# The gate's modulation summed on VectorE alone, with the low parts of the weights on GpSimd, in the last two stages

## The chip, the cores and the metric

The kernel runs on one core of a Trainium2 chip. The metric is the device time of one execution in microseconds (us); lower is better. Before the change three runs gave a median of 1195.83 us (1193.9 to 1196.08).

## What is computed

One step of a diffusion backbone over 384 tokens of width 2048 (256 of a sample, 128 of a prompt): an adaLN modulation, one wide projection, a state-space branch and an attention branch, and a gated way back. The last part of it is what the change is about:

```
mod = silu(cond) @ w_ada + b_ada             # cond: 2 vectors; w_ada: 2048 x 6144
shift, scale, gate = split(mod, 3)           # gate: the last 2048 columns of w_ada
...
p_s = ys @ w_ssm_out
p_a = (attn * silu(z_a)) @ w_att_out         # the stage `pa`
merged = sigmoid(g_s) * p_s + sigmoid(g_a) * p_a
return x + gate * (merged @ w_o)             # the stage `wo`
```

All of it is in float32.

## The kernel before

**Products in three parts.** TensorE multiplies float32 by splitting each operand into a high part (rounded to the engine's fast float32 form, `F32R`) and a low part (the rest), and adds three products: high x high, high x low, low x high. The high and low parts of the activations are made once (`hh`, `hl`). Those of the weights are made as they stream in, by `Stream.prep` (L59 to L72): ScalarE copies a piece of 128x512 into `hi` (L70), and VectorE or GpSimd subtracts it from the raw piece to give `lo` (L71), GpSimd where the flag `low_on_pool` is set. The flag is set in the first stage and cleared after it (L895, L949).

**Stages.** After the first stage the work is a list of `blocks`, of which the last are `ps` (8 blocks), `pa` (8) and `wo` (4). A block is made of units of weights (one DMA of 512 KB each, four raw buffers), a unit of two halves; one half is called a step here. A `pa` step is 12 matmuls on 128x384 in `mode_b` (L192 to L194), first the six for one PSUM bank, then the six for the other; a `wo` step is 9 matmuls on 128x512 in `mode_a` (L203 to L205), three for each of three banks. A `pa` block has 4 steps, a `wo` block 16, so the gate's step counter `t` runs from 0 to 31 in `pa` and from 32 to 95 in `wo`. The pool `psm` of the products has three banks, `psb` for everything else five. The weights are prepared two steps ahead (`st.upto`, L1445), into four buffers of `hi` and four of `lo`.

**What VectorE evicts.** At the end of a `pa` block (`evac`) VectorE twice computes `tgl = (tgl + 1) * PSUM` and adds it to `ms`, the merged activations; later `split` makes `hh` and `hl` of `ms`. At the end of a `wo` block it multiplies three banks by the gate `gt` into `yt` and adds the input `xt`.

**The gate before.** `gate_step(t)` (L1348) is called once a step in these stages. The first 1024 columns of the gate are summed on TensorE: eight groups of four float32 matmuls with the two conditioning vectors (`ct`, 32 columns wide) as the stationary operand, each of the four in another 32 rows of one bank (L1379); `gate_rows` then adds the bias (`bg`), splits the result and spreads it over the 128 partitions with matmuls by `sel` (L1399). The other 1024 columns are summed on VectorE: for each of 16 blocks of 128 rows of `w_ada` and each of the two vectors one `scalar_tensor_tensor` on 128x512, `acs = gw * ct + acs` (L1365, recorded as L155, the line of the helper); `gate_sums` splits `acs` and spreads and sums it over the partitions with matmuls by a matrix of ones (L1416). The table `GATE` gives the step of each of these 32 blocks, from 26 to 84.

**Order.** Each engine runs its instructions in the order in which the program is written; loads are issued from SyncE's queue, also in order. Generators in `Background` (merging, gate sums) advance by one `yield` a step. The helpers `tt`, `ts` and `stt` (L146 to L155) record VectorE's instructions under their own lines.

Of the kernel before, what the change touches and what calls it, by code (L numbers as in the profile page):

```python
# [6 lines left out]
F32 = mybir.dt.float32  # L7
F32R = mybir.dt.float32r
I32 = mybir.dt.int32
AF = mybir.ActivationFunctionType  # L10
OP = mybir.AluOpType
AX = mybir.AxisListType
# [3 lines left out]
D = 2048  # L16
# [10 lines left out]
def f(ap):  # L27
    return ap.bitcast(F32)


def dram(ap, off, dims):
    return bass.AP(tensor=ap.tensor, offset=ap.offset + off, ap=[list(d) for d in dims])
# [94 lines left out]
def hybrid(ctx, tc, a):  # L127
    nc = tc.nc
    V, S, PE, GP, SP = nc.vector, nc.scalar, nc.tensor, nc.gpsimd, nc.sync
# [13 lines left out]
    def bank():  # L143
        return psb.tile([128, 512], F32, name="bk")

    def tt(o, x, y, op, eng=V):  # L146
        return eng.tensor_tensor(o, x, y, op=op)  # L147

    def ts(o, x, s1, op0, s2=None, op1=None, eng=V):
        if op1 is None:  # L150
            return eng.tensor_scalar(o, x, s1, None, op0=op0)
        return eng.tensor_scalar(o, x, s1, s2, op0=op0, op1=op1)  # L152

    def stt(o, x, s, y, op0, op1):
        return V.scalar_tensor_tensor(o, x, s, y, op0=op0, op1=op1)  # L155
# [740 lines left out]
    i = 0  # L896
# [333 lines left out]
    def enter(kind):  # L1230
        nonlocal kvt
        if kind == "v":
            bg.finish(g_zs)
            zsx.close()
            v = vx.enter_context(pool("vp"))
            M["v"] = [v.tile([128, 1024], F32, name=f"v{r}") for r in range(4)]
            SP.dma_start(M["v"][3], dram(a["cache_v"], 0, [[1024, 128], [1, 1024]]))
        elif kind == "ga":
            pre = prex.enter_context(pool("pre"))
            for k, dims in (("B", [2, 32, 16]), ("C", [4, 2, 2, 64]), ("U", [16, 96]), ("D", [16, 16])):  # L1240
                prefetched[k] = pre.tile([128] + dims, F32, name="pre" + k)
            g_pre.append(bg.add(ssm_read(1, prefetched), True))
        elif kind == "k":
            bg.finish([g_ssm])
            sspx.close()
            prex.close()
            msp = ent(pool("msp", "right"))
            M["ms"] = [msp.tile([128, TOK], F32, name=f"ms{k}") for k in range(16)]
            ts(qwc, qwc, 0.125, OP.mult)
            kv = kvx.enter_context(pool("kv", "right"))  # L1250
            M["kS"] = [kv.tile([128, 384], F32, name=f"kS{j}") for j in range(8)]
            M["kP"] = [kv.tile([128, 128], F32, name=f"kP{j}") for j in range(8)]
            M["qT"] = [kv.tile([128, 384], F32, name=f"qT{j}") for j in range(8)]
            at = atx.enter_context(pool("at", "right"))
            kvt = kvtx.enter_context(pool("kvt", bufs=2))
            g_qk.append(bg.add(context_keys()))
            M["att"] = bg.add(attention(at, M["kS"], M["kP"], M["qT"], M["v"], M["qT"],
                                      M["vd"], M["aT"]))
        elif kind == "act":
            M["zs"], M["ys"] = {}, {}  # L1260
            M["ysg"] = bg.add(split_ys(), True)
        elif kind == "glu":
            bg.finish([M["ysg"]])
            for k in range(2):
                load_glu(k)
        elif kind == "ps":
            bg.finish(g_qk)
            kvtx.close()
            g_za.append(bg.add(gate_att(), True))
        elif kind == "pa":  # L1270
            bg.finish([M["att"]] + g_za)
            atx.close()
            kvx.close()
            vx.close()
            M["gp"] = gp = gx.enter_context(pool("gp", "right"))
            M["gt"] = gp.tile([128, 2, D], F32, name="gt")

            pick = gp.tile([128, 2], F32, name="pick")
            V.tensor_reduce(pick, ident.rearrange("p (g x) -> p x g", x=32)[:, 0:2], axis=AX.X, op=OP.add)
            M["sel"] = gp.tile([128, 3, 128], F32R, name="sel")  # L1280
            V.tensor_copy(M["sel"][:, 0:2], pick.unsqueeze(2).to_broadcast([128, 2, 128]))
            ts(M["sel"][:, 2], ident, 0.0, OP.mult, 1.0, OP.add)
            M["bg"] = gp.tile([128, D], F32, name="bg")
            GP.memset(M["bg"], 0.0)
            for n in range(2):
                SP.dma_start(M["bg"][0:2 - n, 1024 * n:1024 * n + 1024], dram(a["b_ada"], 4096 + 1024 * n, [[0, 2 - n], [1, 1024]]))
            M["tg"] = []
            for k in range(2):
                load_tg(k)
        elif kind == "wo":  # L1290
            g_mg.append(bg.add(merge(range(8, 16), 3), True))
# [55 lines left out]

    def gate_step(t):  # L1348

        for kt in range(32):
            if GATE[kt] - 6 == t and kt % 2 == 0:
                w = gaw[16 + kt // 2] = M["gp"].tile([128, 2, 512], F32, name="gw", bufs=5)
                n, k = divmod(kt, 16)
                SP.dma_start(w, dram(a["w_ada"], 128 * k * 6144 + 5120 + 512 * n, [[6144, 128], [128 * 6144, 2], [1, 512]]))
            if GATE[kt] == t:
                n, k = divmod(kt, 16)  # L1360
                if k == 0:
                    gaw["acc"] = M["gp"].tile([128, 2, 512], F32, name="acs", bufs=1)
                for m in range(2):
                    o = gaw["acc"][:, m]
                    stt(o, gaw[16 + kt // 2][:, kt % 2], ct[:, k, m:m + 1],  # L1365
                        o if k else M["bg"][:, 1024 + 512 * n:1536 + 512 * n], OP.mult, OP.add)
                if k == 15:
                    bg.add(gate_sums(2 + n, gaw["acc"]), True)
        if t % 2 == 0 and t < 32:
            w = gaw[t // 2] = M["gp"].tile([128, 2, 512], F32, name="gw", bufs=5)  # L1370
            n, u = divmod(t // 2, 8)
            SP.dma_start(w, dram(a["w_ada"], 256 * u * 6144 + 4096 + 512 * n, [[6144, 128], [128 * 6144, 2], [1, 512]]))
        quad, r = divmod(t - 8, 4)
        if r == 0 and 0 <= quad < 8:
            n, u = divmod(quad, 4)
            if u == 0:
                gaw["p"] = bank()
            for g in range(4):
                PE.matmul(gaw["p"][32 * g:32 * g + 32, :], ct[:, 4 * u + g, :], gaw[2 * quad + g // 2][:, g % 2],  # L1379
                          start=u == 0, stop=u == 3)  # L1380
            if u == 3:
                bg.add(gate_rows(n, gaw["p"]), True)

    def gate_rows(n, p):

        acc = M["gp"].tile([128, 512], F32, name="acc", bufs=1)
        h = M["gp"].tile([128, 512], F32R, name="gh", bufs=2)
        l = M["gp"].tile([128, 512], F32R, name="gl", bufs=2)
        yield -1
        tt(acc, p, M["bg"][:, 512 * n:512 * n + 512], OP.add)  # L1390
        yield -1
        S.activation(h, acc, AF.Copy)
        yield -1
        tt(l, acc, f(h), OP.subtract)
        for m in range(2):
            yield -1
            p = bank()
            for i, part in enumerate((h, l)):
                PE.matmul(p, M["sel"][:, m], part, start=i == 0, stop=i == 1)  # L1399
            yield -1  # L1400
            S.activation(M["gt"][:, m, 512 * n:512 * n + 512], p, AF.Copy)

    def gate_sums(n, acc):

        parts = []
        for m in range(2):
            parts.append([M["gp"].tile([128, 512], F32R, name=x, bufs=2) for x in ("gh", "gl")])
            S.activation(parts[m][0], acc[:, m], AF.Copy)
        yield -1
        for m in range(2):  # L1410
            tt(parts[m][1], acc[:, m], f(parts[m][0]), OP.subtract)
        for m in range(2):
            yield -1
            p = bank()
            for i, part in enumerate(parts[m]):
                PE.matmul(p, M["sel"][:, 2], part, start=i == 0, stop=i == 1)  # L1416
            yield -1
            S.activation(M["gt"][:, m, 512 * n:512 * n + 512], p, AF.Copy)

    gaw = {}  # L1420
    GATE = [26 + k * 60 // 32 for k in range(32)]
    BUD = {"gs": 2.05, "v": 2.1, "ga": 2.05, "za": 2.05}
    ACT = {"glu": act, "pa": act, "ps": act2, "wo": merged}
    entered, gt_ = set(), 0
    for kind, c0, nk, units in blocks:
        if kind not in entered:
            enter(kind)
            entered.add(kind)
# [58 lines left out]
```

## Time and profile before

| what | value |
|---|---|
| median of three runs | 1195.83 us |
| the profiled execution, its own time | 1188.56 us |
| its span, first to last instruction | 1186.8 us |
| mean granted clock of TensorE | 0.997 |
| TensorE (PE) busy | 1144.7 us, 96% |
| VectorE (DVE) busy | 834.2 us, 70% |
| ScalarE (ACT) busy | 519.6 us, 44% |
| GpSimd (POOL) busy | 176.3 us, 15% |

The profile is of one execution. Busy times are shares of the whole span and hide that stages have different limits. TensorE's matmuls are pipelined, so a matmul's own length (0.33 us on 128x384) is about twice the distance to the next one. PEld are TensorE's weight loads, which overlap its matmuls. In the rows, a line such as `acs<-gw,ct,acs` names the tile written and the tiles read. Tiles `m` and `bk` are in PSUM, all others here in SBUF.

### The profile page before, as it was taken

What the parts mean: (1) busy time and instruction counts of PE and PEld (TensorE: products, weight loads), DVE (VectorE), ACT (ScalarE), POOL (GpSimd) and SP (SyncE); (2) the same over time, 40 slices, a digit from 0 to 9 for tenths busy, and PEclk for the clock granted to TensorE, in tenths of its full rate; (3) what the DMA queues carried; (4) which work ended last, traced back from release to release, by engine and by line L of the source; (5) the groups of instructions that cost most, each with busy time, mean ns of one, the idle gap of its engine ahead of it and who ended that gap; (6) DMA issues with size and microseconds to landing.
All of it is one profiled execution on the core that took longest, in us unless ns stands there. A gap on an engine that the chain in (4) does not pass through costs nothing.

```text
span 1186.8 us, 19637 instructions
## 1 busy us (share of the span) xinstructions
PE 1144.7 (96%) x7215; PEld 1011.2 (85%) x7215; DVE 834.2 (70%) x1960; ACT 519.6 (44%) x978; POOL 176.3 (15%) x150
## 2 busy tenths in 40 slices
PE   4899999999999999999999999998999999999997
PEld 3699999998998888989999888876787998878886
DVE  4465555666899984789998533587788756687873
ACT  4343333354643356463335644556444433343332
POOL 2356555663100000000000001110100000000000
PEclk9999999999999999999999999999999999999999
DMA  9987777568456476427444264446553258886771
GB/s 307 323 267 230 253 250 248 156 170 228 156 125 188 134 150 154 129 83 175 148 155 142 72 200 138 116 132 221 161 163 124 93 167 266 273 293 218 222 231 66
DMA packets 216116, 217.37 MB, mean 183 GB/s; under 512 B 64618, under 2 KB 170690, under 8 KB 215637
## 3 DMA queue, kind: packets, MB, share of 16 engines
q1 hardware_dynamic: 213940, 212.73, 59.3%
q0 software_dynamic: 1184, 3.18, 0.8%
q8 instruction: 57, 0.93, 0.3%
q10 hardware_dynamic: 896, 0.21, 0.1%
q14 instruction: 39, 0.31, 0.1%
HBM read 197.90 MB, written 16.87 MB: 181 GB/s over the span
## 4 chain that ended last, share of the span: by engine, by line
PE 87%; DVE 5%; ACT 3%; DMA 2%; issue 2%; SPq 1%; POOL 0%; ACTq 0%; DVEq 0%; POOLq 0%
PE m L192 11%; PE m L194 11%; PE m L193 11%; PE m L203 9%; PE m L204 9%; PE m L205 9%; PE m L861 6%; PE m L862 5%; PE m L863 5%; PE bk L733 2%; PE bk L478 1%; PE bk L604 1%; PE bk L607 1%; PE bk L1032 1%; DMA raw<-in_w_in_dram 1%
## 5 line engine op out<-in xcount | busy, mean ns | idle before, releaser
L70 ACT ACTIVATE hi<-raw 128x512 fp32r<-128x512 f32 x464 | 287.4, 629 | 338.8 <-PE m L193 123.9
L71 DVE TENSOR_TENSOR lo<-raw,hi 128x512 fp32r<-128x512 f32 x368 | 250.2, 687 | 154.2 <-ACT hi L70 151.3
L192 PE MATMUL m<-hh,hi 128*128 128x384 f32 x832 | 285.3, 343 | 10.7 <-DVE ms L155 2.9
L194 PE MATMUL m<-hh,lo 128*128 128x384 f32 x832 | 278.9, 335 | 0.2
L193 PE MATMUL m<-hl,hi 128*128 128x384 f32 x832 | 278.4, 335 | 0.0
L203 PE MATMUL m<-hi,hh 128*128 128x512 f32 x480 | 189.9, 396 | 0.0
L205 PE MATMUL m<-hi,hl 128*128 128x512 f32 x480 | 187.3, 390 | 0.0
L204 PE MATMUL m<-lo,hh 128*128 128x512 f32 x480 | 187.1, 390 | 0.0
L192 PEld LDWEIGHTS m<-hh,hi 128*128 128x128 f32 x832 | 156.2, 188 | 22.7 <-ACT hi L70 5.4
L194 PEld LDWEIGHTS m<-hh,lo 128*128 128x128 f32 x832 | 156.2, 188 | 0.9 <-DVE lo L71 0.9
L193 PEld LDWEIGHTS m<-hl,hi 128*128 128x128 f32 x832 | 156.3, 188 | 0.1
L71 POOL TENSOR_TENSOR lo<-raw,hi 128x512 fp32r<-128x512 f32 x96 | 124.5, 1307 | 111.4 <-ACT hi L70 107.2
L861 PE MATMUL m<-hh,hi 128*128 128x384 f32 x384 | 132.8, 346 | 5.1 <-DVE ua L925 2.6
L863 PE MATMUL m<-hh,lo 128*128 128x384 f32 x384 | 129.3, 337 | 0.2 <-DVE lo L71 0.2
L862 PE MATMUL m<-hl,hi 128*128 128x384 f32 x384 | 129.2, 336 | 0.3 <-POOL hl L147 0.3
L203 PEld LDWEIGHTS m<-hi,hh 128*128 128x128 f32 x480 | 90.1, 188 | 21.5 <-ACT hi L70 1.4
L205 PEld LDWEIGHTS m<-hi,hl 128*128 128x128 f32 x480 | 90.1, 188 | 19.1
L204 PEld LDWEIGHTS m<-lo,hh 128*128 128x128 f32 x480 | 90.2, 188 | 18.1 <-DVE lo L71 0.3
L861 PEld LDWEIGHTS m<-hh,hi 128*128 128x128 f32 x384 | 72.5, 189 | 14.0 <-issue 5.7
L862 PEld LDWEIGHTS m<-hl,hi 128*128 128x128 f32 x384 | 72.6, 189 | 0.8 <-POOL hl L147 0.5
L863 PEld LDWEIGHTS m<-hh,lo 128*128 128x128 f32 x384 | 72.5, 189 | 0.4 <-DVE lo L71 0.4
L147 POOL TENSOR_TENSOR rm<-rn,mhalf 128x24 f32<-128x24 f32 x4 | 18.1, 4512 | 355.0 <-DVE rn L152 355.0
(270 smaller groups left out, 1274.0 us busy)
## 6 DMA issues: line engine op xcount, KB each, us to landing
raw<-in_w_in_dram SPq DMA_DIRECT2D x160, 512.0 KB, 3.9
wa<-in_w_ada_dram SPq DMA_DIRECT2D x32, 1024.0 KB, 7.7
gw<-in_w_ada_dram SPq DMA_DIRECT2D x32, 512.0 KB, 5.6
raw<-in_w_o_dram SPq DMA_DIRECT2D x32, 512.0 KB, 6.2
raw<-in_w_ssm_out_dram SPq DMA_DIRECT2D x16, 512.0 KB, 3.4
raw<-in_w_att_out_dram SPq DMA_DIRECT2D x16, 512.0 KB, 5.6
raw<-in_w_glu_dram SPq DMA_DIRECT2D x8, 512.0 KB, 4.5
tgs<-sg SPq DMA_DIRECT2D x16, 192.0 KB, 1.9
```

Of the source, the lines that this page charges most:

```text
L70: self.nc.scalar.activation(h, t, AF.Copy)
L71: (self.nc.gpsimd if self.low_on_pool else self.nc.vector).tensor_tensor(l, t, f(h), op=OP.subtract)
L192: PE.matmul(o, wh[:, kk, w], xh[q][:, j, :], start=first and hb == 0 and kk == 0, stop=False)
L193: PE.matmul(o, wh[:, kk, w], xl[q][:, j, :], start=False, stop=False)
L194: PE.matmul(o, wl[:, kk, w], xh[q][:, j, :], start=False, stop=last and hb == 1 and kk == 1)
L203: PE.matmul(ps[r], xh[q][:, j, tk], wh, start=first and hb == 0, stop=False)
L204: PE.matmul(ps[r], xh[q][:, j, tk], wl, start=False, stop=False)
L205: PE.matmul(ps[r], xl[q][:, j, tk], wh, start=False, stop=last and hb == 1)
L733: PE.matmul(pab[b][32 * (k % 4):32 * (k % 4) + 32, 0:128 * nk], ct[:, kt, :], wa[s, i][:, k, :], start=kt < 4, stop=kt >= 12)
L861: PE.matmul(o, wh[:, w], hh[q][:, j, :], start=kk == 0, stop=False)
L862: PE.matmul(o, wh[:, w], hl[q][:, j, :], start=False, stop=False)
L863: PE.matmul(o, wl[:, w], hh[q][:, j, :], start=False, stop=kk == nk - 1)
```

## The change

The whole gate, all 2048 columns, is now summed on VectorE: 64 blocks of rows and columns, two instructions each, spread by a new table `GATE` over steps 6 to 87. The products on TensorE, `gate_rows` and the two columns of `sel` that it used are gone; the matrix of ones is a tile of its own (`one`). The gate's loads, 32 of 512 KB as before, are all issued six steps ahead of the first use. The flag `low_on_pool` is set in `pa` and `wo`, so GpSimd makes the low parts there. The flag also stands in the budget that `bg.step` is given, which is 1 a step now and was 0.4.

```diff
-            M["sel"] = gp.tile([128, 3, 128], F32R, name="sel")
...
+            M["one"] = gp.tile([128, 128], F32R, name="one")
+            ts(M["one"], ident, 0.0, OP.mult, 1.0, OP.add)
             M["bg"] = gp.tile([128, D], F32, name="bg")
             GP.memset(M["bg"], 0.0)
...
+            SP.dma_start(M["bg"][0:1], dram(a["b_ada"], 4096, [[0, 1], [1, D]]))
...
     def gate_step(t):
-        for kt in range(32):
+        for kt in range(64):
+            n, k = divmod(kt, 16)
             if GATE[kt] - 6 == t and kt % 2 == 0:
...
             if GATE[kt] == t:
...
                 for m in range(2):
                     o = gaw["acc"][:, m]
-                    stt(o, gaw[16 + kt // 2][:, kt % 2], ct[:, k, m:m + 1],
-                        o if k else M["bg"][:, 1024 + 512 * n:1536 + 512 * n], OP.mult, OP.add)
+                    stt(o, gaw[kt // 2][:, kt % 2], ct[:, k, m:m + 1],
+                        o if k else M["bg"][:, 512 * n:512 * n + 512], OP.mult, OP.add)
                 if k == 15:
-                    bg.add(gate_sums(2 + n, gaw["acc"]), True)
-        if t % 2 == 0 and t < 32:
...
-            for g in range(4):
-                PE.matmul(gaw["p"][32 * g:32 * g + 32, :], ct[:, 4 * u + g, :], gaw[2 * quad + g // 2][:, g % 2],
-                          start=u == 0, stop=u == 3)
...
+                    bg.add(gate_sums(n, gaw["acc"]), True)
...
-                PE.matmul(p, M["sel"][:, 2], part, start=i == 0, stop=i == 1)
+                PE.matmul(p, M["one"], part, start=i == 0, stop=i == 1)
...
-    GATE = [26 + k * 60 // 32 for k in range(32)]
+    GATE = [6 + k * 80 // 64 + (k // 16) for k in range(64)]
...
     for kind, c0, nk, units in blocks:
+        st.low_on_pool = kind in ("pa", "wo")
```

The order of the instructions at three places follows. First VectorE in `pa`, between the evictions of the fourth block and the fifth, before:

```order
L147 TENSOR_TENSOR ms_7904<-ms_7904,tgl 128x384
L155 SCALAR_TENSOR_TENSOR tgl<-tgl,m 128x384
L147 TENSOR_TENSOR ms_7905<-ms_7905,tgl 128x384
L71 TENSOR_TENSOR lo<-raw,hi 128x512 x3
L155 SCALAR_TENSOR_TENSOR hl_105<-ms_7904,hh_101 128x384
L71 TENSOR_TENSOR lo<-raw,hi 128x512
L155 SCALAR_TENSOR_TENSOR hl_105<-ms_7905,hh_101 128x384
L155 SCALAR_TENSOR_TENSOR tgl<-tgl,m 128x384
```

and at the same place now:

```order
L147 TENSOR_TENSOR ms_7904<-ms_7904,tgl 128x384
L155 SCALAR_TENSOR_TENSOR tgl<-tgl,m 128x384
L147 TENSOR_TENSOR ms_7905<-ms_7905,tgl 128x384
L155 SCALAR_TENSOR_TENSOR acs<-gw,ct,acs 128x512 x6
L155 SCALAR_TENSOR_TENSOR hl_105<-ms_7904,hh_101 128x384
L155 SCALAR_TENSOR_TENSOR acs<-gw,ct,acs 128x512 x2
L155 SCALAR_TENSOR_TENSOR hl_105<-ms_7905,hh_101 128x384
L155 SCALAR_TENSOR_TENSOR tgl<-tgl,m 128x384
```

Four lows have gone from between the two evictions, and eight gate sums stand there. Second, VectorE in `wo`, from the eviction of its first block to that of its second, now:

```order
L147 TENSOR_TENSOR yt<-m,gt 128x512 x3
L147 TENSOR_TENSOR yt<-yt,xt 128x512 x3
L155 SCALAR_TENSOR_TENSOR acs<-gw,ct,bg 128x512 x2
L155 SCALAR_TENSOR_TENSOR acs<-gw,ct,acs 128x512 x24
L147 TENSOR_TENSOR yt<-m,gt 128x512 x3
```

Before, 16 lows stood among fewer gate sums there; now 26 gate sums stand between two evictions with nothing else. Third, the end of GpSimd's queue, as a piece of the difference (- before, + now):

```order
 L147 TENSOR_TENSOR rm<-rn,mhalf 128x24 x4
-L1284 MEMSET bg 128x2048
-L1483 UNCONDITIONAL_BRANCH
-L1483 ISA
+L1280 MEMSET bg 128x2048
+L71 TENSOR_TENSOR lo<-raw,hi 128x512 x94
```

GpSimd had nothing to do after the clearing of `bg`; it now makes 94 lows.

## Rows read from the trace of the kernel before

**Rows 1.** Busy in `pa`, `wo`: length; PE, PEld, DVE, ACT, POOL (count); granted clock; DMA

```profile
970.00:1044.00 74.00, 74.00 (x433) 67.29 (x433) 46.98 (x82) 25.76 (x46) 0.00 (x0) 1.00 0.81 262
1046.00:1179.00 133.00, 133.00 (x592) 108.26 (x592) 95.68 (x150) 44.51 (x73) 0.00 (x0) 1.00 0.63 207
```

**Rows 2.** VectorE groups from 964 us: line, instruction, count | busy, mean ns | idle, releaser

```profile
L71 DVE TENSOR_TENSOR lo<-raw,hi 128x512 fp32r<-128x512 f32 x96 | 64.7, 688 | 46.9 <-ACT hi L70 46.7
L155 DVE SCALAR_TENSOR_TENSOR acs<-gw,ct,acs 128x512 f32<-128x512 f32 x60 | 42.2, 745 | 0.0
L155 DVE SCALAR_TENSOR_TENSOR tgl<-tgl,m 128x384 f32<-128x384 f32 x16 | 8.8, 550 | 10.0 <-PE m L194 10.0
L147 DVE TENSOR_TENSOR yt<-m,gt 128x512 f32<-128x512 f32 x12 | 8.2, 692 | 8.2 <-PE m L205 8.2
```

**Rows 3.** TensorE in order of time, `pa`: start, length, instruction; eight matmul records of the gate

```profile
985.79 0.33 PE L192 MATMUL m<-hh,hi 128*128 128x384 f32 x1
...
987.35 0.33 PE L192 MATMUL m<-hh,hi 128*128 128x384 f32 x1
...
987.96 1.06 PE L1379 MATMUL bk<-gw,ct 128*32 128x512 f32 x8
...
990.65 0.33 PE L192 MATMUL m<-hh,hi 128*128 128x384 f32 x1
```

**Rows 4.** TensorE in order of time, `wo`

```profile
1051.40 0.39 PE L203 MATMUL m<-hi,hh 128*128 128x512 f32 x1
...
1053.44 0.39 PE L203 MATMUL m<-hi,hh 128*128 128x512 f32 x1
```

**Rows 5.** Groups of the spreading matmuls, from 964 us to the end

```profile
L1399 PE MATMUL bk<-gh,sel 128*128 128x512 f32 x4 | 1.7, 418 | 0.0
L1416 PE MATMUL bk<-gh,sel 128*128 128x512 f32 x4 | 1.6, 391 | 0.0
```

**Rows 6.** The page: loads of the gate weights, count, size, us to landing

```profile
gw<-in_w_ada_dram SPq DMA_DIRECT2D x32, 512.0 KB, 5.6
```

**Rows 7.** GpSimd, then VectorE, in order of time, first stage

```profile
266.02 1.30 POOL L71 TENSOR_TENSOR lo<-raw,hi 128x512 fp32r<-128x512 f32 x1 [1.37 <-ACT hi L70]
266.39 1.34 DVE L155 SCALAR_TENSOR_TENSOR zs<-sg,zs 128x384 f32<-128x384 f32 x1
```

**Rows 8.** GpSimd, then VectorE, in order of time, 210 to 218 us

```profile
214.27 1.62 POOL L71 TENSOR_TENSOR lo<-raw,hi 128x512 fp32r<-128x512 f32 x1
214.27 2.98 POOL L71 TENSOR_TENSOR lo<-raw,hi 128x512 fp32r<-128x512 f32 x2
213.40 1.32 DVE L147 TENSOR_TENSOR cm<-fw,pw 128x384 f32<-128x384 f32 x1
215.58 0.52 DVE L147 TENSOR_TENSOR fw<-fw,cm 128x192 f32<-128x192 f32 x1
```

**Rows 9.** VectorE, then GpSimd, in order of time, 61 to 64 us

```profile
61.88 2.06 DVE L147 TENSOR_TENSOR zs<-m,zs 128x384 f32<-128x384 f32 x4
61.93 1.29 POOL L71 TENSOR_TENSOR lo<-raw,hi 128x512 fp32r<-128x512 f32 x1 [3.71 <-ACT hi L70]
```

**Rows 10.** Pairs of VectorE instructions that follow each other, in order of time

```profile
978.75 1.28 DVE L71 TENSOR_TENSOR lo<-raw,hi 128x512 fp32r<-128x512 f32 x2
1060.28 1.41 DVE L155 SCALAR_TENSOR_TENSOR acs<-gw,ct,acs 128x512 f32<-128x512 f32 x2
```

**Rows 11.** VectorE, then TensorE, in order of time, 892 to 895 us

```profile
893.47 1.00 DVE L155 SCALAR_TENSOR_TENSOR ms<-ms,m 128x384 f32<-128x384 f32 x2
894.06 0.44 PE L192 MATMUL m<-hh,hi 128*128 128x384 f32 x1 [2.90 <-DVE ms L155]
```

**Rows 12.** A pause of TensorE, and its granted clock (PEclk) after it

```profile
32.37 0.69 PE L861 MATMUL m<-hh,hi 128*128 128x384 f32 x1 [2.63 <-DVE ua L925]
32.00:34.00 2.00, 1.64 (x5) 0.56 1.09 349
34.00:36.00 2.00, 2.00 (x22) 0.59 1.10 354
```

More of the change, by code (lines that the diff above doesn't have):

```diff
@@ L1276, in enter @@
             M["gt"] = gp.tile([128, 2, D], F32, name="gt")
-            pick = gp.tile([128, 2], F32, name="pick")
-            V.tensor_reduce(pick, ident.rearrange("p (g x) -> p x g", x=32)[:, 0:2], axis=AX.X, op=OP.add)
-            M["sel"] = gp.tile([128, 3, 128], F32R, name="sel")
-            V.tensor_copy(M["sel"][:, 0:2], pick.unsqueeze(2).to_broadcast([128, 2, 128]))
-            ts(M["sel"][:, 2], ident, 0.0, OP.mult, 1.0, OP.add)
+            M["one"] = gp.tile([128, 128], F32R, name="one")
+            ts(M["one"], ident, 0.0, OP.mult, 1.0, OP.add)
             M["bg"] = gp.tile([128, D], F32, name="bg")
             GP.memset(M["bg"], 0.0)
-            for n in range(2):
-                SP.dma_start(M["bg"][0:2 - n, 1024 * n:1024 * n + 1024], dram(a["b_ada"], 4096 + 1024 * n, [[0, 2 - n], [1, 1024]]))
+            SP.dma_start(M["bg"][0:1], dram(a["b_ada"], 4096, [[0, 1], [1, D]]))
             M["tg"] = []
@@ L1348, in gate_step @@
     def gate_step(t):
-        for kt in range(32):
+        for kt in range(64):
+            n, k = divmod(kt, 16)
             if GATE[kt] - 6 == t and kt % 2 == 0:
-                w = gaw[16 + kt // 2] = M["gp"].tile([128, 2, 512], F32, name="gw", bufs=5)
-                n, k = divmod(kt, 16)
-                SP.dma_start(w, dram(a["w_ada"], 128 * k * 6144 + 5120 + 512 * n, [[6144, 128], [128 * 6144, 2], [1, 512]]))
+                w = gaw[kt // 2] = M["gp"].tile([128, 2, 512], F32, name="gw", bufs=5)
+                SP.dma_start(w, dram(a["w_ada"], 128 * k * 6144 + 4096 + 512 * n, [[6144, 128], [128 * 6144, 2], [1, 512]]))
             if GATE[kt] == t:
-                n, k = divmod(kt, 16)
                 if k == 0:
@@ L1364, in gate_step @@
                     o = gaw["acc"][:, m]
-                    stt(o, gaw[16 + kt // 2][:, kt % 2], ct[:, k, m:m + 1],
-                        o if k else M["bg"][:, 1024 + 512 * n:1536 + 512 * n], OP.mult, OP.add)
+                    stt(o, gaw[kt // 2][:, kt % 2], ct[:, k, m:m + 1],
+                        o if k else M["bg"][:, 512 * n:512 * n + 512], OP.mult, OP.add)
                 if k == 15:
-                    bg.add(gate_sums(2 + n, gaw["acc"]), True)
-        if t % 2 == 0 and t < 32:
[L1370 to L1377, printed above, removed]
-            for g in range(4):
-                PE.matmul(gaw["p"][32 * g:32 * g + 32, :], ct[:, 4 * u + g, :], gaw[2 * quad + g // 2][:, g % 2],
-                          start=u == 0, stop=u == 3)
[L1381 to L1401, printed above, removed]
+                    bg.add(gate_sums(n, gaw["acc"]), True)
     def gate_sums(n, acc):
```

## The prediction

> **What bounds the kernel now.** Read the stages apart first. In `pa` and in `wo` TensorE is busy for the whole of both stretches, 74.00 of 74 us and 133.00 of 133 us, at a granted clock of 1.00 (the level of 2.4 GHz), while VectorE is busy for 46.98 and 95.68 us and GpSimd not at all [rows 1]. So in these two stages any time of TensorE that goes shortens the kernel, and work moved between VectorE and GpSimd is free only as long as neither makes TensorE wait. Then TensorE in order of time gives the lengths of a step (half a unit, twelve matmuls in `pa`, nine in `wo`). In `pa` nine matmuls take 987.35 - 985.79 = 1.56 us, so twelve take 2.08 us [rows 3]; in `wo` a step is 1053.44 - 1051.40 = 2.04 us [rows 4]. The groups of VectorE then say what it does in that time: lows at 688 ns and gate sums `acs` at 745 ns are the two large ones [rows 2]. Last, the first stage has to be read, though the change doesn't touch it: it is the only place where GpSimd makes lows today, and its rows tell what VectorE does beside them.
>
> **The change part by part.**
>
> *TensorE's gate products go: a gain.* A group of four products (eight matmul records, 1.06 us) stands between matmuls of a `pa` block; from the `L192` at 987.35 to that at 990.65 lie twelve ordinary matmuls and the group, 3.30 us, of which the twelve are 2.08 us [rows 3]. A group costs 1.22 us, and all eight groups lie where TensorE is never idle: 8 x 1.22 = **9.8 us less**.
>
> *Spreading the sums over the partitions: nothing.* Eight matmuls with `sel` go, eight with `one` come, at 418 and 391 ns a record [rows 5].
>
> *The gate's loads: nothing.* The same 32 loads of 512 KB are spread evenly. Each is issued 6 steps (about 12 us) ahead of its use and lands in 5.6 us [rows 6]; five buffers of two products each last 12.5 steps, and that is the cover. The larger budget of the background has no effect here: its generators in these stages give only negative numbers, which cost none of it.
>
> *94 lows move to GpSimd, 64 more gate sums come to VectorE.* By busy time this would be harmless: VectorE loses 64.7 us of lows and gains 64 x 0.745 = 47.7 us [rows 2], and a low of 1.30 us on GpSimd [rows 7] is shorter than a step. But the two engines don't run these instructions side by side. Beside a low that runs from 266.02 to 267.32 us, VectorE starts a `scalar_tensor_tensor` on 128x384 with both tensors in SBUF at 266.39; it takes 1.34 us and ends at 267.73, which is 0.41 us after the low [rows 7]. The other way round, a low waits for VectorE: `cm` ends at 214.72 and the low beside it, 1.62 us long, at 215.89, 1.17 us later; `fw` ends at 216.10 and the next low at 217.25, 1.15 us later [rows 8]. They take turns. Where one of VectorE's inputs is in PSUM nothing of the kind is seen: four additions from `m` take 2.06 us in a row beside a low of 1.29 us [rows 9].
>
> The Trainium skill says the same in SBUF — State Buffer, section Who interferes with whom: a VectorE instruction with two SBUF inputs contends with a GpSimd instruction that reads SBUF, and whichever comes first holds the shared ports for its whole instruction. This case's trace agrees in kind, but its turns are shorter than the instructions (1.15 us of a 1.30 us low). By that rule the sum would be that of the last rival, 1247 us, by the rows it is 1213 us.
>
> So I price **turns**. A low: 1.15 us [rows 8]. A VectorE instruction right behind a low: 0.41 us for 384 columns [rows 7], hence 0.41 x 512/384 = 0.55 us for 512 (an estimate). One right behind another of VectorE: the pair of `acs` takes 1.41 us, so 1.41 - 0.745 = 0.67 us [rows 2, 10]; the pair of 512-column subtractions 1.28 - 0.69 = 0.60 us [rows 2, 10]; 384 columns (2.06 - 0.55)/3 = 0.50 us [rows 2, 9]. One instruction per low gets the short price, the rest the long one. What reads PSUM (`tgl`, `yt<-m`) fits beside the lows and is costed at nothing.
>
> In `pa` the new sums run in steps 6 to 31: 26 steps, 26 x 2.08 = 54.1 us of TensorE. On the shared ports stand 26 lows, 29.9 us, and 64 VectorE instructions: 40 `acs`, 14 additions to `ms` and 8 `hl` (384 columns), 2 `gl`. 26 of 64 are short, 41%, so an `acs` costs 0.62, a 384 0.46, a `gl` 0.58 us: 24.8 + 10.2 + 1.2. Together 66.1 us, **12.0 us too many**.
>
> In `wo` they run in steps 32 to 87: 56 x 2.04 = 114.2 us. 56 lows are 64.4 us; 109 VectorE instructions are 88 `acs` at 0.61 (51% are short), 8 `hl` at 0.45, 4 `gl` and 9 additions of `xt` at 0.575: 53.6 + 3.6 + 7.5. Together 129.1 us, **14.9 us too many**.
>
> TensorE pays for that at the ends of blocks. A `pa` block holds two of three PSUM banks, so the next block's second half needs the bank that VectorE has yet to read; in `wo` all three. The eviction stands in VectorE's queue behind the sums that are late. The trace has one such wait already: 2.90 us of TensorE for `ms` [rows 11]. Next late would be the lows themselves, made only two steps ahead.
>
> The sum: 12.0 + 14.9 - 9.8 = **+17.1 us**. Against the profiled execution that is 1188.56 + 17.1 = 1205.7 us; that one ran 7.3 us below the median of the three runs, 1195.83 us, so the forecast in the terms of the median is **1213 us**.
>
> *Bounds.* If every VectorE instruction got the short price, `pa` would be 62.0 us and `wo` 123.3 us, +7.2 us in all; the lead of two steps can hide up to 4.2 us once, +3 us: 1199 us. If the evictions that read PSUM found no low to run beside, 14 x 0.55 + 9 x 0.69 = 13.9 us come on top [rows 2]: 1227 us. And a long pause of TensorE can cost more than itself: after one of 2.63 us in the first stage the granted clock was 0.56 and 0.59 for the next 4 us, between its two levels, which loses some 1.7 us [rows 12]; three of these make 1232 us. After the 2.90 us of [rows 11] the matmuls ran at once at their usual length, so I leave this out of the sum.
>
> **The rivals.**
>
> *Faster: the turns don't decide.* If VectorE's gate sums ran beside the lows as PSUM additions do, only TensorE's groups would count: 1195.83 - 9.8 = 1186 us. For it: VectorE's and GpSimd's busy times each fit a step. Against it: [rows 7, 8]. It holds if the ports are free for over 0.9 us of each step beyond what I count. Chance 0.08.
>
> *No change: only `pa` pays.* A `wo` step leaves 2.04 - 1.15 = 0.89 us beside a low, and the sums alone (88 in 56 steps, 1.57 a step) need 1.57 x 0.55 = 0.86 us at the short price. If the rest hides, 12.0 - 9.8 = +2.2 us: 1198 us. Against it: 21 more instructions want the same ports, and one short price per low is all that taking turns gives. Chance 0.06.
>
> *Slower by more: uncovered evictions and a lower clock*, 1227 to 1232 us as bounded above. For it: in `pa` VectorE has no slack left, so an eviction may meet an empty GpSimd; [rows 12]. Against it: with lows waiting all the time there is nearly always one to run beside. Chance 0.13.
>
> *Slower by far: each holds the ports for its whole instruction.* 26 lows at 1.30 us, 40 `acs` at 0.745, 22 of 384 columns at 0.55, 2 `gl` at 0.69 are 77.1 us in `pa`, 23.0 too many; in `wo` 56 lows, 88 `acs`, 8 `hl`, 13 others at the same prices are 151.8 us, 37.6 too many; 60.6 - 9.8 = +50.8 us, 1247 us [rows 2, 7]. Against it: the ends in [rows 8]. Chance 0.03. It is the rule of the Trainium skill named above, at its word.
>
> **How the numbers follow.** The forecast, 0.70, has a range of its own of 1203 to 1227 us. To leave out no more than 2 in 10 I go down to 1198, where the lower bound and the second rival lie, and up to 1231; what is left out is the first rival, the last, and the far end of the third. A measurement of this kernel can tell 0.2%, 2.4 us, from no change. Faster is the first rival, 0.08; within 0.2% the second, 0.06; slower the forecast and the last two, 0.86.
>
> **What would show it.** Right: the records of `L1379` are gone; `acs` lasts well over 745 ns on the mean, up to about 1.9 us where it meets a low, and `lo` on GpSimd over 1.30 us; TensorE is no longer busy throughout `pa` and `wo` but pauses a few us at ends of blocks, released by VectorE's `tgl` and `yt`, some 27 us in all. Six of the eight groups stood in `pa`, so `pa` is about 12.0 - 7.3 = 5 us longer and `wo` 14.9 - 2.4 = 12 us. Wrong: `acs` stays at 745 ns beside lows, or TensorE pauses on the lows themselves or on loads and not on evictions, or the pauses come to less than 10 us.

## The result, and the profile after

The changed kernel takes 1215.72 us in the median of four runs (1212.88 to 1218.29), the kernel before, run beside it, 1195.42 us: a ratio of 1.0176, 95% interval 1.0153 to 1.0199. It is slower by 20.3 us; forecast was slower by 17.1, at 1213 us.

The profiled execution took 1216.46 us. Its busy times, from the page:

```profile
PE 1151.2 (95%) x7151; PEld 1021.4 (84%) x7151; DVE 893.4 (74%) x1928; ACT 520.1 (43%) x980; POOL 320.9 (26%) x244
```

GpSimd went from 176.3 to 320.9 us, VectorE from 834.2 to 893.4 us, though its 94 lows went away. The same by stage, `pa` (here from the first `tgl` to the first `L203`) and `wo` (from there to the last `L203`), in the columns of [rows 1]:

```profile
985.30:1058.10 72.80, 64.82 (x347) 63.37 (x346) 69.81 (x77) 24.16 (x43) 42.24 (x29) 0.93 0.67 216
1058.10:1207.60 149.50, 138.80 (x586) 112.16 (x586) 135.19 (x127) 46.46 (x78) 96.35 (x62) 0.97 0.60 201
```

TensorE, which was busy throughout both stages, now is for 64.82 of 72.80 us and 138.80 of 149.50, and its mean granted clock is 0.93 and 0.97 where it was 1.00. The groups of VectorE and GpSimd from 960 us on answer to [rows 2]:

```profile
L71 POOL TENSOR_TENSOR lo<-raw,hi 128x512 fp32r<-128x512 f32 x94 | 144.2, 1541 | 188.4 <-ACT hi L70 187.8
L155 DVE SCALAR_TENSOR_TENSOR acs<-gw,ct,acs 128x512 f32<-128x512 f32 x120 | 134.9, 1191 | 0.0
L155 DVE SCALAR_TENSOR_TENSOR tgl<-tgl,m 128x384 f32<-128x384 f32 x16 | 8.7, 545 | 9.0 <-PE m L194 9.0
L147 DVE TENSOR_TENSOR yt<-m,gt 128x512 f32<-128x512 f32 x12 | 7.7, 686 | 14.1 <-PE m L205 13.9 <-ACT hi L70 0.2
```

A gate sum lasts 1191 ns on the mean, 1853 at most, and took 745 before; a low on GpSimd lasts 1541 ns and took about 1300 in the first stage. Evictions that read PSUM kept their lengths, 545 and 686 ns. What TensorE waited for, in total, times, longest:

```profile
PE m L192 <- DVE tgl L155: 7.9, 3, 4.6
PE m L203 <- DVE yt L147: 5.9, 2, 5.0
PE m L204 <- POOL lo L71: 1.7, 1, 1.7
PE m L203 <- DVE tgl L155: 1.5, 2, 1.0
```

Nearly all of it is released by VectorE's evictions `tgl` and `yt`, once by a low. How the two engines stand to each other is seen in any piece where both are busy; here GpSimd (one low, and the same with the next), then VectorE (two gate sums, and the next two, which begin with the second of them), around 1111 us:

```profile
1111.38 1.29 POOL L71 TENSOR_TENSOR lo<-raw,hi 128x512 fp32r<-128x512 f32 x1 [1.76 <-ACT hi L70]
1111.38 2.99 POOL L71 TENSOR_TENSOR lo<-raw,hi 128x512 fp32r<-128x512 f32 x2 [1.76 <-ACT hi L70]
1110.76 2.46 DVE L155 SCALAR_TENSOR_TENSOR acs<-gw,ct,acs 128x512 f32<-128x512 f32 x2
1111.42 3.50 DVE L155 SCALAR_TENSOR_TENSOR acs<-gw,ct,acs 128x512 f32<-128x512 f32 x2
```

The first low ends at 1112.67 us, and the sum that waited for it at 1110.76 + 2.46 = 1113.22, 0.55 us later. The second low ends at 1114.37, 1.15 us after that sum; the next sum ends at 1114.92, 0.55 us after the second low. These are the two prices of the forecast. They are also the commonest in both stages: of the gate sums that end behind a low, 15 of 22 in `pa` and 34 of 53 in `wo` do so after 0.53 to 0.57 us, and of the lows that end behind one of VectorE's instructions with two tensors in SBUF, 22 of 36 and 46 of 54 do so after 1.13 to 1.17 us.

One pause, at the end of a `pa` block, in order of time: two gate sums and the eviction behind them on VectorE, and TensorE's first matmul after the pause:

```profile
1004.22 2.41 DVE L155 SCALAR_TENSOR_TENSOR acs<-gw,ct,acs 128x512 f32<-128x512 f32 x2
1007.02 0.54 DVE L155 SCALAR_TENSOR_TENSOR tgl<-tgl,m 128x384 f32<-128x384 f32 x1
1007.62 0.44 PE L192 MATMUL m<-hh,hi 128*128 128x384 f32 x1 [3.12 <-DVE tgl L155]
```

TensorE in the stretches from then on (length, busy time and matmuls, granted clock, share of the DMA engines, GB/s):

```profile
1006.00:1008.00 2.00, 0.38 (x2) 1.00 0.15 52
1008.00:1010.00 2.00, 2.00 (x9) 0.59 0.34 91
1010.00:1012.00 2.00, 2.00 (x8) 0.55 0.78 197
1012.00:1014.00 2.00, 2.00 (x14) 1.00 0.90 309
```

The eviction starts only when two sums of 2.41 us and an `hl` are done, TensorE has waited 3.12 us for the bank, and then for some 4 us the granted clock is 0.59 and 0.55, that is, mostly at the lower of the two levels (1.2 GHz). Pauses in these two stages come to 18.5 us: the 17.0 us above and 1.5 us of the gate's own spreading matmuls.

### The profile page after: what moved, and what is told of

It is laid out like the page before. It is cut to its first block, busy times and chain, and to the rows that moved or that the text cites. A ratio compares the mean times of both kernels' runs of the same rounds, so it can differ in the third digit from the quotient of the medians.

```text
span 1214.6 us, 19599 instructions
## 1 busy us (share of the span) xinstructions
PE 1151.2 (95%) x7151; PEld 1021.4 (84%) x7151; DVE 893.4 (74%) x1928; ACT 520.1 (43%) x980; POOL 320.9 (26%) x244
## 4 chain that ended last, share of the span: by engine, by line
PE 75%; DVE 11%; DMA 5%; issue 4%; ACT 3%; SPq 1%; POOL 1%; DVEq 0%; ACTq 0%; POOLq 0%
PE m L192 10%; PE m L193 10%; PE m L194 10%; PE m L203 6%; PE m L204 6%; PE m L205 6%; PE m L861 6%; DVE acs L155 5%; PE m L862 5%; PE m L863 5%; PE bk L733 2%; DMA raw<-in_w_in_dram 2%; PE bk L478 1%; PE bk L604 1%; DVE yt L147 1%
## 5 line engine op out<-in xcount | busy, mean ns | idle before, releaser
L71 POOL TENSOR_TENSOR lo<-raw,hi 128x512 fp32r<-128x512 f32 x190 | 269.1, 1425 | 299.9 <-ACT hi L70 295.1
L71 DVE TENSOR_TENSOR lo<-raw,hi 128x512 fp32r<-128x512 f32 x274 | 187.2, 688 | 112.3 <-ACT hi L70 109.6
L203 PE MATMUL m<-hi,hh 128*128 128x512 f32 x480 | 191.7, 399 | 7.4 <-DVE yt L147 5.9
L192 PEld LDWEIGHTS m<-hh,hi 128*128 128x128 f32 x832 | 159.0, 191 | 28.3 <-DVE tgl L155 9.3
L194 PEld LDWEIGHTS m<-hh,lo 128*128 128x128 f32 x832 | 158.8, 191 | 0.9 <-DVE lo L71 0.9
L193 PEld LDWEIGHTS m<-hl,hi 128*128 128x128 f32 x832 | 159.0, 191 | 0.1
L155 DVE SCALAR_TENSOR_TENSOR acs<-gw,ct,acs 128x512 f32<-128x512 f32 x120 | 134.9, 1191 | 0.0
L203 PEld LDWEIGHTS m<-hi,hh 128*128 128x128 f32 x480 | 91.1, 190 | 29.1 <-issue 5.9
L861 PEld LDWEIGHTS m<-hh,hi 128*128 128x128 f32 x384 | 72.6, 189 | 13.9 <-issue 5.9
L862 PEld LDWEIGHTS m<-hl,hi 128*128 128x128 f32 x384 | 72.9, 190 | 0.8 <-POOL hl L147 0.5
```

What stands on the lines that cost most here:

```text
L71: (self.nc.gpsimd if self.low_on_pool else self.nc.vector).tensor_tensor(l, t, f(h), op=OP.subtract)
L192: PE.matmul(o, wh[:, kk, w], xh[q][:, j, :], start=first and hb == 0 and kk == 0, stop=False)
L193: PE.matmul(o, wh[:, kk, w], xl[q][:, j, :], start=False, stop=False)
L194: PE.matmul(o, wl[:, kk, w], xh[q][:, j, :], start=False, stop=last and hb == 1 and kk == 1)
L203: PE.matmul(ps[r], xh[q][:, j, tk], wh, start=first and hb == 0, stop=False)
L861: PE.matmul(o, wh[:, w], hh[q][:, j, :], start=kk == 0, stop=False)
```

## The experiments

Theory: a low on GpSimd and a VectorE instruction with two tensors in SBUF take turns, and the turns do not fit a step. Rivals: VectorE's longer queue is late by itself (the 64 added sums); GpSimd's lows are late by themselves.

**The sums kept in PSUM.** The accumulator of the gate sums is moved out of SBUF into two banks of PSUM, and `gate_sums` reads it there. So 120 of the 128 sums read one tensor from SBUF and one from PSUM; the first of each sixteen, eight in all, still reads `gw` and the bias `bg`, both in SBUF, and writes to PSUM.

```diff
-                    gaw["acc"] = M["gp"].tile([128, 2, 512], F32, name="acs", bufs=1)
+                    gaw["acc"] = [bank(), bank()]
...
-                    o = gaw["acc"][:, m]
+                    o = gaw["acc"][m]
...
-            S.activation(parts[m][0], acc[:, m], AF.Copy)
+            S.activation(parts[m][0], acc[m], AF.Copy)
...
-            tt(parts[m][1], acc[:, m], f(parts[m][0]), OP.subtract)
+            tt(parts[m][1], acc[m], f(parts[m][0]), OP.subtract)
```

> The changed kernel with the gate's sums `acs` kept in two PSUM banks instead of SBUF, so that each gate sum on VectorE has one SBUF tensor and one PSUM tensor as inputs. Count, order and engine of every instruction stay. If the two engines take turns on instructions with two SBUF inputs: the sums no longer meet the lows, `acs` is back near 0.75 us and `lo` near 1.30 us, TensorE's pauses go, and what is left is the gain of the eight groups, 1195.4 - 9.8, so 1185 to 1189 us. If VectorE's longer queue alone makes the evictions late: as many instructions of the same length, so no change against the changed kernel, 1211 to 1219 us. If GpSimd's lows are late by themselves: also 1211 to 1219 us.

Measured: 1186.67 us, 0.9943 of the kernel before (0.9925 to 0.9960). Its groups (the sums are now `bk<-gw,ct,bk`), from 960 us on:

```profile
L71 POOL TENSOR_TENSOR lo<-raw,hi 128x512 fp32r<-128x512 f32 x94 | 125.4, 1339 | 191.2 <-ACT hi L70 191.0
L155 DVE SCALAR_TENSOR_TENSOR bk<-gw,ct,bk 128x512 f32<-128x512 f32 x120 | 81.2, 746 | 7.1 <-DMA gw<-in_w_ada_dram 7.1
L147 DVE TENSOR_TENSOR ms<-ms,tgl 128x384 f32<-128x384 f32 x16 | 16.1, 1007 | 0.5
L155 DVE SCALAR_TENSOR_TENSOR bk<-gw,ct,bg 128x512 f32<-128x512 f32 x8 | 11.9, 1530 | 0.0
```

and TensorE's waits:

```profile
PE m L192 <- DVE tgl L155: 0.6, 2, 0.4
PE m L204 <- POOL lo L71: 0.3, 1, 0.3
```

The sums last 746 ns although 94 lows run beside them, and the pauses are all but gone. An addition with both tensors in SBUF, `ms<-ms,tgl`, still lasts 1007 ns where it took about 560: the turns are still there, but now they fit. The eight first sums write to PSUM like the others but read both tensors from SBUF, and last 1530 ns: what counts is where an instruction reads, not where it writes. This settles the theory against both rivals, and the kernel is faster than either of the two under study.

The run also gives the cost by stage, since it has the same instructions in the same order as the changed kernel. With the stages bounded as above, TensorE (length, busy time and matmuls, granted clock, share of the DMA engines, GB/s) in the kernel before:

```profile
976.60:1044.00 67.40, 67.40 (x395) 1.00 0.81 262
1044.00:1179.30 135.30, 135.30 (x603) 1.00 0.64 208
```

and in the kernel with sums in PSUM:

```profile
985.70:1047.00 61.30, 60.66 (x347) 1.00 0.77 255
1047.00:1180.80 133.80, 133.38 (x587) 1.00 0.67 225
```

| | `pa`, us | `wo`, us |
|---|---|---|
| before | 67.4 | 135.3 |
| changed | 72.8 | 149.5 |
| sums in PSUM | 61.3 | 133.8 |
| changed less sums in PSUM | 11.5 | 15.7 |
| too many by the forecast | 12.0 | 14.9 |

**Lows on VectorE, the whole gate there too.**

```diff
-        st.low_on_pool = kind in ("pa", "wo")
+        st.low_on_pool = False
```

> The changed kernel with the lows of `pa` and `wo` left on VectorE; the whole gate is still summed there. If taking turns is the cost: VectorE has its own queue only. In steps 6 to 31 that is 40 sums at 0.67, 26 lows at 0.60, 36 instructions of 384 columns at 0.50 and 2 at 0.60, 61.6 us against 54.1 us of TensorE, some 7 us too many; in `wo` it fits. With 9.8 us gained: 1190 to 1196 us. If the 64 added sums are the cost, whoever makes the lows: no better than the changed kernel, 1213 us or more, since VectorE has more to do still.

Measured: 1192.96 us, ratio 0.9995 (0.9977 to 1.0013). Groups and TensorE's waits:

```profile
L155 DVE SCALAR_TENSOR_TENSOR acs<-gw,ct,acs 128x512 f32<-128x512 f32 x120 | 84.4, 744 | 0.0
L71 DVE TENSOR_TENSOR lo<-raw,hi 128x512 fp32r<-128x512 f32 x101 | 68.4, 686 | 20.6 <-ACT hi L70 20.4
```

```profile
PE m L192 <- DVE tgl L155: 3.0, 2, 2.1
PE m L204 <- DVE lo L71: 1.1, 2, 0.5
```

With 128 gate sums and the lows in one queue, VectorE is late by a few us (pauses of 4.5 us in the two stages, two thirds of it in `pa`) where TensorE waits 18.5 us in the changed kernel. By stage it is 65.2 us in `pa` and 135.4 in `wo`, 3.9 and 1.6 us more than with sums in PSUM; the text said some 7 us in `pa` and none in `wo`. Both kinds last what they did before, 744 and 686 ns. So it is not the number of sums.

**Lows on GpSimd, the old gate.** The kernel before with one added line.

```diff
     for kind, c0, nk, units in blocks:
+        st.low_on_pool = kind in ("pa", "wo")
```

> The kernel before with one thing changed: GpSimd makes the lows of `pa` and `wo`. The gate is summed as before, half on TensorE. If taking turns is the cost: the turns fit. In `pa` 32 lows at 1.15 and few sums; in `wo` 56 lows are 64.4 us, 58 sums some 35 us and 21 others some 11 us, 110 us against 114 us of TensorE. So no change, 1193 to 1199 us, with `acs` lengthened to over 1 us all the same. If lows on GpSimd come too late by themselves (1.3 us and more instead of 0.69): over 1205 us, with TensorE pausing on `lo`.

Measured: 1193.80 us, ratio 1.0007 (0.9989 to 1.0024). Groups, then the two stages in the columns of [rows 1]:

```profile
L71 POOL TENSOR_TENSOR lo<-raw,hi 128x512 fp32r<-128x512 f32 x94 | 136.0, 1454 | 175.1 <-ACT hi L70 173.3 <-DMA raw<-in_w_att_out_dram 0.8 <-DMA gw<-in_w_ada_dram 0.8
L155 DVE SCALAR_TENSOR_TENSOR acs<-gw,ct,acs 128x512 f32<-128x512 f32 x60 | 74.2, 1299 | 3.5 <-DMA gw<-in_w_ada_dram 3.5
```

```profile
970.00:1044.00 74.00, 74.00 (x434) 67.47 (x433) 42.15 (x50) 24.79 (x44) 38.78 (x30) 1.00 0.80 258
1046.00:1179.00 133.00, 133.00 (x599) 108.76 (x598) 106.86 (x94) 47.92 (x82) 94.44 (x63) 1.00 0.67 223
```

A sum lasts 1299 ns here, more than in the changed kernel, and a low 1454, but TensorE is busy for all of both stages. Taking turns by itself costs nothing as long as there are turns enough in a step; neither the move of the lows nor the added sums alone is what cost 20 us, but both together.

**One stage at a time.** GpSimd makes the lows in `pa` only, or in `wo` only.

```diff
-        st.low_on_pool = kind in ("pa", "wo")
+        st.low_on_pool = kind == "pa"
```

> The changed kernel with GpSimd making the lows in `pa` only; in `wo` VectorE makes them. By the turns `pa` pays 12.0 us and `wo`, where VectorE's own queue fits a step, nothing: 1194.2 + 12.0 - 9.8, so 1194 to 1200 us, with TensorE pausing at the ends of `pa` blocks alone. If the cost of the changed kernel lay in `wo`: 1185 to 1189 us.

> The changed kernel with GpSimd making the lows in `wo` only. Against the run with all lows on VectorE, 1193.0 us, the turns in `wo` add 14.9 us: 1204 to 1211 us, with pauses of TensorE at the ends of `wo` blocks. If most of the cost of the changed kernel lay in `pa`: 1193 to 1198 us.

Measured: `pa` only 1200.13 us, ratio 1.0046 (1.0028 to 1.0063); `wo` only 1204.89 us, ratio 1.0088 (1.0067 to 1.0110). TensorE's waits, `pa` only:

```profile
PE m L192 <- DVE tgl L155: 7.9, 3, 4.6
PE m L204 <- DVE lo L71: 1.1, 2, 0.5
```

and `wo` only:

```profile
PE m L203 <- DVE yt L147: 4.7, 2, 4.0
PE m L192 <- DVE tgl L155: 3.0, 2, 2.1
PE m L203 <- DVE tgl L155: 1.4, 2, 0.8
```

Each stage pays for itself, at the ends of its own blocks. `pa` costs 1200.13 - 1186.67 = 13.5 us against the run with sums in PSUM (the text said 12.0, and the run ends just above its range; by the stages of the profiles it is 11.6 us in `pa` and 2.4 in `wo`, where VectorE's own queue was said to fit); `wo` costs 1204.89 - 1192.96 = 11.9 us against lows on VectorE (said: 14.9). Beside these two runs the kernel before took 1194.56 us, beside the two that they are set against 1194.24.

**What a pause costs.** The kernel before with needless additions ahead of three `pa` evictions.

```diff
+        if kind == "pa" and c0 in (512, 1024, 1536):
+            for _ in range(11):
+                tt(M["gt"][:, 1, 1536:2048], M["bg"][:, 0:512], M["bg"][:, 0:512], OP.add)
         evac(kind, c0, ps)
```

> The kernel before with eleven needless additions of 128x512 (0.60 us each) in VectorE's queue ahead of the evictions of three `pa` blocks; they write a part of `gt` that is written again later. Each delays an eviction, so that TensorE pauses by about 3 us three times. If a pause costs only itself: 9 to 10 us, 1203 to 1207 us, granted clock 1.00 after each. If the granted clock falls after a pause as it did at some pauses of the changed kernel: one to three spells of 3 to 7 us at half speed on top, 1.5 to 3.5 us each, so 1207 to 1215 us.

Measured: 1218.32 us, ratio 1.0215 (1.0188 to 1.0241), longer than either case said, because the delay was: one after another the additions take 7.94 us, 0.72 each and not 0.60. The additions, the first matmul after the first pause, and TensorE's waits over the three:

```profile
1002.07 7.94 DVE L147 TENSOR_TENSOR gt<-bg 128x512 f32<-128x512 f32 x11
1010.53 0.69 PE L192 MATMUL m<-hh,hi 128*128 128x384 f32 x1 [4.92 <-DVE tgl L155]
```

```profile
PE m L192 <- DVE tgl L155: 15.6, 3, 5.8
```

TensorE after the first pause, in the same columns as for the changed kernel:

```profile
1008.00:1011.00 3.00, 0.47 (x1) 0.60 0.00 0
1011.00:1014.00 3.00, 3.00 (x14) 0.50 0.49 130
1014.00:1017.00 3.00, 3.00 (x16) 0.76 0.97 295
```

The first matmul after the other two pauses lasts 0.69 us as well. Over the stage, as bounded above:

```profile
985.70:1076.20 90.50, 74.90 (x395) 0.89 0.61 195
```

The three pauses are 15.6 us, but the kernel is longer by 1218.32 - 1194.24 = 24.1 us (1194.24 is the kernel before beside these runs). In the stage alone TensorE is busy for 74.90 us where the same 395 matmuls took 67.40, 7.5 us more: that is TensorE at about half its clock for some us after each pause. The last 1 us lies elsewhere and is not traced. The case in which a pause costs only itself is out.

## Why the prediction was right, and where it was not

**TensorE's groups, 9.8 us less: right in kind, some 2 us too much.** Where the turns fit, `pa` shrank by 67.4 - 61.3 = 6.1 us and `wo` by 1.5, 7.6 us together, as the medians have it too (1194.24 - 1186.67). TensorE's busy time in the two stages fell from 202.70 to 194.04 us, 8.7 us, so a group was worth some 1.1 us on the mean and not the 1.22 read off one place. Another 1.1 us is idle time of TensorE that is left (0.64 and 0.42 us).

**The turns: right.** Prices 0.55 and 1.15 us, taken from the first stage and one of them scaled from 384 to 512 columns, came back unchanged in `pa` and `wo`. They gave 12.0 + 14.9 = 26.9 us too many; measured are 11.5 + 15.7 = 27.2 us. By stage the forecast was some 5 us longer in `pa` and 12 in `wo`; measured are 72.8 - 67.4 = 5.4 and 149.5 - 135.3 = 14.2 us. (The 0.60 us for a second 512-column subtraction is 1.28 - 0.69 = 0.59 by its rows, which moves nothing.) The rival in which each engine holds the ports for its whole instruction (1247 us) is out by the same rows: a low beside a waiting sum needs 1.15 us of its 1.29. That rival was the rule of the Trainium skill's SBUF — State Buffer, section Who interferes with whom, at its word; this trace agrees that the two take turns, and not with the length of a turn. The rival in which the turns don't decide (1186 us) is out, and the run with sums in PSUM shows what it would have been: 1186.67 us.

**Who is late: right.** The pauses stand at the ends of blocks and end with `tgl` and `yt`; a low was late once for 1.7 us. Evictions that read PSUM were costed at nothing, and kept their lengths.

**Pauses alone: wrong, though the sum held.** The text put all of the 27 us into pauses, and said of the granted clock "I leave this out of the sum". Pauses are 18.5 us, 0.9 of which stands in the run with sums in PSUM too, so 17.6 us of the 27.2; the other 9.6 us are matmuls at the lower clock after them (TensorE is busy for 203.62 us of the two stages, and for 194.04 with the sums in PSUM). The pause run shows that such a spell comes on top of the pause where VectorE has nothing to catch up on. In the changed kernel the whole is none the less what the turns alone gave, and VectorE's rows show why. In `pa` it is idle for 3.0 us of 72.8, and in `wo`, until the last gate sum has been split, for 0.4 us of 135.1:

```profile
1058.10:1193.20 135.10, 134.71 (x126) 0.96 0.66 222
```

So VectorE's queue, its turns included, sets the length of both stages, and it goes on working off what it is behind with while TensorE is slow: the spell stands in place of a later pause. That follows from these rows; a kernel with the same turns and no spells was not run. The upper bound of 1232 us, which added spells on top, would then be too high for a kernel that is behind all the time.

**The rival "only `pa` pays": wrong.** `wo` paid more than `pa`.

## What to carry to other kernels

Before moving elementwise work from VectorE to GpSimd, sort VectorE's instructions by where the tensors that they read are: those that read two from SBUF run one at a time with GpSimd's, and their turns and GpSimd's must fit into the step together, while busy times that fit side by side say nothing. Prices for that can be had from any stage in which the two already run together. An accumulator in PSUM takes an instruction out of the contest.

## What the runs showed of the hardware that was not expected

The scalar operand doesn't count. The gate sum reads `gw` and, as one scalar per partition, `ct`, both in SBUF; with the accumulator in PSUM it lasts 746 ns beside lows, as it did alone.

The same pause may or may not lower the clock. A wait for `kr` stands in code that the change doesn't touch. In the profiled execution of the kernel before, the first matmul after it, and TensorE from 828 us on:

```profile
828.83 0.44 PE L192 MATMUL m<-hh,hi 128*128 128x384 f32 x1 [2.73 <-ACT kr L1176]
```

```profile
828.00:832.00 4.00, 3.17 (x17) 1.00 0.95 274
```

In that of the changed kernel, after a pause of the same length:

```profile
834.48 0.69 PE L192 MATMUL m<-hh,hi 128*128 128x384 f32 x1 [2.75 <-ACT kr L1176]
```

```profile
834.00:836.00 2.00, 1.52 (x5) 0.57 0.81 218
```

Full clock the one time, 0.57 the other. Over the whole way up to the first `tgl`, in which both kernels run the same 6121 matmuls, before:

```profile
27.00:976.60 949.60, 930.12 (x6121) 1.00 0.58 171
```

and after the change:

```profile
27.00:985.30 958.30, 936.92 (x6121) 0.99 0.57 170
```

TensorE is busy for 6.8 us longer with the same matmuls. The 8.7 us between the two have nothing to do with the change: two kernels with the old gate, the one with lows on GpSimd and the one with the added pauses, reach the first `tgl` at 983.2 and 985.7 us. The first of them has the same 67.4 and 135.3 us in `pa` and `wo` as the kernel before, and its profiled execution took 1195.21 us, 6.7 us longer, which is the 6.6 us that it comes later to the first `tgl`. This is why the profiled execution before, 1188.56 us, lay 7.3 us below its median, and why a sum over a profile has to be set against that profile's own time.
